# A two-layer hybrid DeltaNet / S5 / MLA / MoE block on one core: a timeline simulation as the list scheduler's machine, and another merge order for the first mixer

## The chip, the cores and the metric

The kernel runs on one NeuronCore of a Trainium2 chip. The metric is the device time of one execution in microseconds (us), as the median of several runs.

## The reference, cut to what matters

There are 256 latent tokens and 256 context tokens of width 1024, and two layers. Every sub-layer is RMS norm, a shift and scale that come from a conditioning vector through a large matrix (`ada_w`, 2 x 1024 x 6144), the work itself, and a gated residual.

```
for i in range(2):
    sh1, sc1, g1, sh2, sc2, g2 = adaln(c, ada_w[i], ada_b[i])        # and the same for c_ctx
    h_l, h_c = modulate(x, ...), modulate(ctx, ...)
    if i == 0: o_c, o_l = mixer_ab(h_c, h_l, ...)   # gated DeltaNet (4 heads, two directions) beside S5 (32 groups)
    else:      _, o_l = mixer_mla(h_c, h_l, ...)    # latent attention, 8 heads
    x = x + g1 * o_l
    x = x + g2 * grouped_moe(modulate(x, ...))      # 16 experts, top 2, f32 weights
    # in layer 0 the same two lines for ctx
return rmsnorm(x, final_norm_g)
```

The DeltaNet heads project the input to q, k, v, z, pass q, k, v through a convolution over 5 tokens, normalize k, build decay matrices for each of 4 token tiles and 2 directions, solve a triangular system in each tile, and scan over the tiles. The S5 groups are a linear recurrence over time with a gated output (`glu`).

## The kernel before, in words

**Stages.** The kernel is written in a tile framework: each statement issues one instruction on one engine, and the framework adds the semaphores and the buffer slots. In the order of the program:

1. `norm0` and the first third of layer 0's conditioning (`ada_gen(0, 0)`), then the input projection of the S5 part (`proj_u`) beside the first quarter of the S5 tables.
2. The first mixer's projections, tables, S5 recurrences and decay matrices, as five streams that are merged (below), with the last 72 loads of `ada_w` as the fifth.
3. Triangular solves and the scan (`solve`, `scan`, `dn_out`).
4. The output projection of layer 0 (`out_proj0`), its router, and its 16 experts (`experts0`, three fp32r passes on TensorE for each product).
5. The attention of layer 1 (`prep`, `keys`, `scores`, `values`), its output projection (`out_proj1`), the router, the experts (`experts1`, f32, two experts side by side), and the last norm.

**The merge.** `merge(order, *gens)` at the end of stage 1 takes one digit of `ORDER` after the other and runs the generator of that number up to its next `yield`; what is left goes round robin. The streams are:

- 0: `s5_run(0)` to `s5_run(3)` and `glu()`. `s5_run(q)` waits (by yielding) until the tables of quarter q are there, multiplies (`U`, `Eq`), scans on VectorE, multiplies again (`Fq`, `XC`, `Tq`) and transposes. `glu` makes four blocks; each of them holds a tile of the tag `sq` (L973) until its result is stored (L977).
- 1: `s5_tables(1)` to `s5_tables(3)`: factors `Fq`, `Eq`, and then `Tq`, which goes out to DRAM in 4 transfers (`kdd`, L579) and comes back in 8 (L583), all on the queue of SyncE (SP).
- 2: `gates`, `norm_k`, `decays` (8 steps, two for each token tile), `inverses`. A step of `decays` stores its matrices (`egd` on SP at L864, `dcd` and `atd` on ScalarE's queue at L865 and L867). `inverses` loads them back in 4 transfers on SP (`x<-atd`, L873), copies them (L874), and then runs a chain of 31 pairs on VectorE (L880, L882). It stores the result (`xvd`, L887 and L888).
- 3: `proj_k`, `proj_z`, `proj_q`, `proj_v`: 16 blocks of 128 channels, 24 matmuls each, with a load of weights (L608), a split into two fp32r parts (L602, L603) and, but for z, a convolution on VectorE (L742).
- 4: `loads`: 8 stores of zeros, then `ada_gen` for the other parts of the conditioning, 72 steps of one 512 KB load on SP and 2 matmuls (of f32, so 4 records in the trace).

`ORDER` has 224 digits: 50, 30, 30, 24 and 90 of the five streams.

**Behind the merge.** `fetch` loads the decay matrices (`A<-atd`, L1048, on SP), and 16 transfers bring the inverses into `DT` (L1040). Their tiles lie where tiles of the merge lay, so they wait until those are given up.

**The second output projection.** `out_proj1` multiplies in two column halves (`n` = 0, 1; 48 matmuls `ps<-ch,oT` each). Between them it calls `moe_open`, which loads `cols<-modd` (L1323, 8 KB, on ScalarE's queue; in it, each element of 4 bytes has an address of its own) and multiplies it with the router's matrix (`ps<-rw,cols`, 8 matmuls of f32, 16 records).

**What sets the order on an engine.** Each engine runs its instructions in a fixed order, and so does each DMA queue: an instruction whose semaphore has not come holds all those behind it. The framework finds this order when the program is complete. It is a list scheduler: it plays the program on a simulated machine, and whenever an engine of that machine is free it takes the instruction with the lowest number in program order among those whose inputs are ready there. So both matter, the program's order (`ORDER` for the merge) and what the simulated machine holds to be ready. The machine is by default the functional core simulator. With `schedule_with_timeline_sim=True` (L2187) it is a timeline simulation, in which every instruction is a list of events that hold engines, queues and other devices, for which instructions contend. Where the program demands an order, it says so with `issue_after`.

Of the kernel before, what the change touches and what calls it, by code (L numbers as in the profile page):

```python
# [38 lines left out]
ARB = 3  # L39
EA = 0  # L40
HG = (2, 5)
ORDER = "40124430441043014410430044034041140224222234140404134042104340241432100440412304401424034102444031420440134204140344014042231440204144304214040321444142300041204344012034140402430142440423041422241143444000003444432444444444"


def const_arrays():
# [115 lines left out]
def _build(es, tc, I, O):  # L161
# [156 lines left out]
    def merge(order, *gens):  # L318

        for c in order:  # L320
            next(gens[int(c)], None)
        rr(*gens)
# [5 lines left out]
    def seq(*gens):  # L328
        for g in gens:
            yield from g  # L330
# [632 lines left out]
    def glu():  # L963
        gluw = [load_chunk(I["glu_w"][:, n * 256:(n + 1) * 256].rearrange("(k p) n -> p k n", p=128), [128, 4, 256])
                for n in range(2)]
        glub = gp.tile([128, 4], F32, name="glub")
        nc.sync.dma_start(glub, I["glu_b"])
        V.tensor_scalar(glub, glub, 0.5, None, op0=OP.mult)
        for b in range(4):
            p = ps(1)  # L970
            for k in range(4):
                mm(p, gluw[b // 2][:, k, b % 2 * 128:b % 2 * 128 + 128], yT[:, k, :], k == 0, k == 3)
            th = d2.tile([128, 512], F32, tag="sq", bufs=2, name=nm("gth"))  # L973
            S.activation(th, p, AF.Tanh, scale=0.5, bias=glub[:, b:b + 1])
            V.tensor_scalar(th, th, 0.5, 0.5, op0=OP.mult, op1=OP.add)
            V.tensor_tensor(th, yT[:, b, :], th, op=OP.mult)
            G.dma_start(c5d[b], th)  # L977
            yield
# [13 lines left out]
    with tc.issue_after(mark.ins):  # L992
        G.memset(X, 0.0)
        rr(with_loads(proj_u()), s5_tables(0))
    yT = pj.tile([128, 4, 512], F32, tag="uy", name="yT")
    merge(ORDER,
          seq(s5_run(0), s5_run(1), s5_run(2), s5_run(3), glu()),
# [1193 lines left out]
```

## Time and profile before

| what | value |
|---|---|
| median of 3 runs | 1413.93 us (1410.01 to 2414.91) |
| the profiled execution's own time | 1414.94 us |
| its span, first to last instruction | 1412.7 us |
| mean granted TensorE clock | 0.942 of full speed |
| busy: TensorE matmul / VectorE / ScalarE / GpSimd | 1251.5 / 787.6 / 529.6 / 381.0 us |
| moved by DMA | 340.40 MB |

Times in the rows are from the start of the span. The span is one execution; 2.2 us lie around it. PE is TensorE's matmuls, PEld its weight loads, DVE VectorE, ACT ScalarE, POOL GpSimd, SP SyncE; "SPq" and "ACTq" are the instructions that start transfers on those two queues. A row of the timeline has start, length, engine, line, operation, output<-inputs and count, and in square brackets the idle time before it and what ended it.

### The profile page before, as it was taken

The numbers are of one execution on the slowest core, as the hardware profiler recorded it, in microseconds if no ns is written. First come the engines' busy times: TensorE is split into PE (matmuls) and PEld (weight loads), VectorE is DVE, ScalarE is ACT, GpSimd is POOL, SyncE is SP. The second block draws the span as 40 slices with busy tenths as digits, with TensorE's granted clock in tenths as the row PEclk, the third lists the DMA queues.
The fourth block names the chain that finished last, engine by engine and source line by source line (L and its number), as shares of the span: only waits on it lengthen the run. The fifth ranks groups of instructions, "written<-read, shape, count | busy, mean of one in ns | idle before, by whom it ended". The sixth has DMA issues, their size and how long they took to land. (4 is left out here: it accounts for less than half of the span.)

```text
span 1412.7 us, 18172 instructions
## 1 busy us (share of the span) xinstructions
PE 1251.5 (89%) x6716; PEld 847.8 (60%) x6716; DVE 787.6 (56%) x1460; ACT 529.6 (37%) x775; POOL 381.0 (27%) x266
## 2 busy tenths in 40 slices
PE   5889989899788999589999999976999669999996
PEld 1786655555327988457777777744777544444422
DVE  5776756844974465767775577775566151221112
ACT  3312634544112242167776477724365011000100
POOL 1443434320126330334443233353231020000000
PEclk9999999899798999789999999998999779999998
DMA  8713457767488345679999699753034569999980
GB/s 306 257 34 88 155 171 221 225 216 235 149 251 281 131 172 180 273 244 345 377 369 330 227 317 358 283 210 113 32 135 155 194 254 385 398 401 400 399 336 31
DMA packets 201805, 340.40 MB, mean 241 GB/s; under 512 B 31726, under 2 KB 70638, under 8 KB 201201
## 3 DMA queue, kind: packets, MB, share of 16 engines
q1 hardware_dynamic: 171952, 310.97, 62.3%
q10 hardware_dynamic: 23920, 16.95, 3.9%
q0 software_dynamic: 5840, 11.28, 2.2%
q8 instruction: 55, 0.90, 0.3%
q14 instruction: 38, 0.30, 0.1%
HBM read 320.56 MB, written 27.82 MB: 247 GB/s over the span
## 5 line engine op out<-in xcount | busy, mean ns | idle before, releaser
L206 PE MATMUL ps<-hi,sp 128*128 128x512 f32 x816 | 269.5, 404 | 6.0 <-ACT sp L1640 3.7
L1661 DVE TENSOR_TENSOR lo<-ch,hi 128x2048 fp32r<-128x2048 f32 x80 | 185.1, 2330 | 84.6 <-ACT hi L1660 79.8
L1660 ACT ACTIVATE hi<-ch 128x2048 fp32r<-128x2048 f32 x96 | 184.1, 1920 | 80.3 <-PE ps L206 52.8
L206 PEld LDWEIGHTS ps<-hi,sp 128*128 128x128 f32 x816 | 154.0, 190 | 42.7 <-ACT sp L1640 4.4
L206 PE MATMUL ps<-lo,sp 128*128 128x512 f32 x408 | 164.9, 404 | 3.2 <-DVE lo L1661 2.4
L206 PE MATMUL ps<-ch,stat 128*32 128x512 f32 x384 | 93.9, 646 | 31.7 <-DMA ch<-in_ada_w 30.6
L206 PE MATMUL ps<-ch,xT 128*64 128x512 f32 x480 | 119.7, 596 | 0.0
L1661 POOL TENSOR_TENSOR lo<-ch,hi 128x2048 fp32r<-128x2048 f32 x16 | 73.9, 4621 | 160.6 <-ACT hi L1660 160.6
L206 PEld LDWEIGHTS ps<-lo,sp 128*128 128x128 f32 x408 | 77.8, 191 | 26.9 <-DVE lo L1661 8.8
L206 PEld LDWEIGHTS ps<-ch,xT 128*64 128x64 f32 x480 | 36.1, 137 | 66.5 <-issue 65.2
L228 POOL TENSOR_TENSOR frs<-rs,sm 128x1 f32<-128x1 f32 x2 | 1.1, 560 | 259.8 <-DVE rs L227 259.8
L1867 ACT ACTIVATE aT<-ps 128x512 f32<-128x512 f32 x8 | 4.8, 597 | 149.1 <-PE ps L203 149.1
L206 PE MATMUL ps<-ch,aT 128*64 128x512 f32 x240 | 60.0, 596 | 0.7 <-ACTq L1588 0.7
L1880 DVE TENSOR_TENSOR y<-ps,bcm 128x512 f32<-128x512 f32 x16 | 11.1, 691 | 81.8 <-PE ps L206 81.8
L603 POOL TENSOR_TENSOR wl<-raw,wh 128x1024 fp32r<-128x1024 f32 x16 | 38.7, 2417 | 66.2 <-ACT wh L602 66.0
L206 PE MATMUL ps<-hH,wh 128*128 128x512 f32 x128 | 55.0, 430 | 0.0
L206 PEld LDWEIGHTS ps<-ch,stat 128*32 128x32 f32 x384 | 13.6, 112 | 67.7 <-DMA ch<-in_ada_w 35.0
L206 PE MATMUL ps<-hL,wh 128*128 128x512 f32 x128 | 53.8, 420 | 0.0
L206 PE MATMUL ps<-hH,wl 128*128 128x512 f32 x128 | 53.1, 415 | 0.0
L742 DVE SCALAR_TENSOR_TENSOR ac<-ps,convw,ac 128x510 f32<-128x510 f32 (+1 forms) x48 | 35.5, 740 | 23.7 <-ACT ac L738 23.3
L1152 POOL TENSOR_TENSOR ch<-ch,ch 128x512 fp32r<-128x512 f32 (+1 forms) x28 | 31.1, 1127 | 58.3 <-ACT ch L1151 32.3
L206 PE MATMUL ps<-y,sT 128*128 128x512 f32 x80 | 40.9, 642 | 6.4 <-DVE y L1880 2.3
(543 smaller groups left out, 2559.7 us busy)
## 6 DMA issues: line engine op xcount, KB each, us to landing
ch<-in_wg SPq DMA_DIRECT2D x63, 1024.0 KB
ch<-in_wd SPq DMA_DIRECT2D x62, 1024.0 KB
ch<-in_wu SPq DMA_DIRECT2D x61, 1024.0 KB
ch<-in_ada_w SPq DMA_DIRECT2D x88, 512.0 KB
raw<-in_w_in SPq DMA_DIRECT2D x16, 512.0 KB
bcm<-modd ACTq DMA_DIRECT2D x12, 512.0 KB
x<-in_xs SPq DMA_DIRECT2D x8, 512.0 KB
yd<-x SPq DMA_DIRECT2D x8, 512.0 KB
```

The lines of the kernel that those rows point to most:

```text
L206: return T.matmul(out, l, r, start=start, stop=stop)
L228: G.tensor_tensor(out, t, bc(neghalf, [128, n]), op=OP.pow)
L603: eng.tensor_tensor(wl, w, wh.bitcast(F32), op=OP.subtract)
L742: V.scalar_tensor_tensor(ac[:, :, lo:hi], pv[:, :, lo + o:hi + o], convw[:, blk, j:j + 1], ac[:, :, lo:hi], op0=OP.mult, op1=OP.add)
L1152: eng.tensor_tensor(lo, src, hi.bitcast(F32), op=OP.subtract)
L1660: last_split[:] = (S.activation(hi, w, AF.Copy), eng.tensor_tensor(lo, w, hi.bitcast(F32), op=OP.subtract))
L1661: eng.tensor_tensor(lo, w, hi.bitcast(F32), op=OP.subtract))
L1867: S.activation(j.aT.rearrange("p k n -> p (k n)"), p, AF.Copy)
L1880: V.tensor_tensor(j.y[:, nh], p, g2[:, nh * 512:(nh + 1) * 512], op=OP.mult)
```

## The change

`TileContext` gets `schedule_with_timeline_sim=True`, and `ORDER` becomes another string with the same count of each digit. No instruction is added or removed, and no size changes.

```diff
-ORDER = "40124430441043014410430044034041140224222234140404134042104342240341432100440412304401424034102444031420440134204140344014042231440204144304214040321444142300041204344012034140402430142440423041422241143444000003444432444444444"
+ORDER = "34412403430144440044040300242210424344412243010024424111140334104140214400004414102414344410200402240124334343003344404201040010120044140302144444443240404244431011020444414342402413424412004334321404444044442023224044444404144"
...
-    with tile.TileContext(nc) as tc:
+    with tile.TileContext(nc, schedule_with_timeline_sim=True) as tc:
```

## Rows read from the trace of the kernel before

**Rows 1.** The page: the span, TensorE's busy time, and its clock in 40 slices.

```profile
span 1412.7 us, 18172 instructions
...
PE 1251.5 (89%) x6716; PEld 847.8 (60%) x6716; DVE 787.6 (56%) x1460; ACT 529.6 (37%) x775; POOL 381.0 (27%) x266
...
PEclk9999999899798999789999999998999779999998
```

**Rows 2.** Busy time by stretch, one line for each (stretch, its length, then as named).

```profile
core 0: us, PE busy (x) PEld busy (x) DVE busy (x) ACT busy (x) POOL busy (x), PEclk, DMA share, GB/s
58.00:428.00 370.00, 327.00 (x2125) 214.40 (x2124) 250.68 (x506) 130.02 (x227) 120.20 (x92) 0.93 0.59 181
...
365.00:410.00 45.00, 31.42 (x153) 11.81 (x154) 43.16 (x73) 4.63 (x12) 8.71 (x4) 0.81 0.55 180
...
600.00:935.00 335.00, 321.13 (x1446) 248.73 (x1445) 228.89 (x157) 235.06 (x196) 128.86 (x49) 0.98 0.86 306
935.00:1104.00 169.00, 152.48 (x680) 110.96 (x679) 101.19 (x254) 70.53 (x171) 51.37 (x46) 0.94 0.38 138
...
1160.00:1395.00 235.00, 230.16 (x1075) 92.08 (x1074) 43.26 (x81) 19.79 (x32) 0.00 (x0) 1.00 0.92 349
```

**Rows 3.** TensorE's timeline in the merged stretch: some matmuls that came after a wait.

```profile
76.64 1.11 PE L203 MATMUL ps<-cm,w 128*128 128x128 f32 x4 [4.72 <-DVE w L550]
...
191.02 1.09 PE L203 MATMUL ps<-cm,kn 128*128 128x128 f32 x4 [5.43 <-DVE kn L764]
...
272.77 2.04 PE L206 MATMUL ps<-kT 128*128 128x128 f32 x8 [5.03 <-DVE x L855]
...
381.48 1.92 PE L206 MATMUL ps<-ch,stat 128*32 128x512 f32 x4 [3.12 <-DMA ch<-in_ada_w]
...
397.05 1.05 PE L206 MATMUL ps<-ch,stat 128*32 128x512 f32 x4 [1.24 <-DMA ch<-in_ada_w]
```

**Rows 4.** Timelines of SyncE's queue, VectorE and TensorE at the end of the merge.

```profile
338.57 6.68 SPq L199 DMA_DIRECT2D ch<-in_ada_w  x2
345.35 4.21 SPq L873 DMA_DIRECT2D x<-atd  x4
349.66 2.01 SPq L579 DMA_DIRECT2D kdd<-kc  x4
351.77 1.70 SPq L199 DMA_DIRECT2D ch<-in_ada_w  x2
359.52 3.64 SPq L583 DMA_DIRECT2D Tq<-kdd  x8
...
362.80 0.68 DVE L874 COPY x<-x 64x1024 f32<-64x1024 f32 x1
...
408.98 1.05 DVE L886 COPY x<-x 128x1024 f32<-128x1024 f32 x1
...
414.43 4.56 PE L206 MATMUL ps<-yT,ch 128*128 128x512 f32 x10
...
426.59 0.69 DVE L976 TENSOR_TENSOR gth<-yT,gth 128x512 f32<-128x512 f32 x1
...
427.44 0.38 SPq L1048 DMA_DIRECT2D A<-atd  x1
...
430.41 2.04 PE L206 MATMUL ps<-DT,A 128*128 128x128 f32 x8 [4.93 <-DMA A<-atd]
```

**Rows 5.** Timelines of TensorE and ScalarE's queue in the second output projection; one stretch.

```profile
1095.71 8.71 PE L206 MATMUL ps<-ch,oT 128*128 128x512 f32 x36
...
1098.48 0.45 ACTq L1323 DMA_DIRECT2D cols<-modd  x1
...
1117.88 3.57 PE L206 MATMUL ps<-rw,cols 128*128 128x16 f32 x16 [13.46 <-DMA cols<-modd]
1121.29 7.45 PE L206 MATMUL ps<-ch,oT 128*128 128x512 f32 x24
...
1120.00:1130.00 10.00, 10.00 (x41) 8.21 (x41) 1.96 (x4) 0.59 (x1) 0.00 (x0) 0.76 0.00 0
```

More of the change, by code (lines that the diff above doesn't have):

```diff
@@ L41 @@
 HG = (2, 5)
-ORDER = "40124430441043014410430044034041140224222234140404134042104340241432100440412304401424034102444031420440134204140344014042231440204144304214040321444142300041204344012034140402430142440423041422241143444000003444432444444444"
+ORDER = "34412403430144440044040300242210424344412243010024424111140334104140214400004414102414344410200402240124334343003344404201040010120044140302144444443240404244431011020444414342402413424412004334321404044442023224044444404144"
 def const_arrays():
```

## Prediction

> **What bounds the kernel now.** I read the page first. TensorE's matmuls fill 1251.5 of 1412.7 us [rows 1], so 161.2 us of the span are without one, and the change, which takes no instruction away, can only win from those and from stretches at the lower clock. Then I cut the span into stages [rows 2]. In the merged stretch (58 to 428 us) matmuls fill 327.0 of 370.0 us: 43 us are open. In layer 0's experts it is 321.1 of 335, in the attention 152.5 of 169, so 14 and 17 us are open there. In layer 1's experts 230.2 of 235 us are filled, beside a DMA share of 0.92: that stage ends with its weights, and order gains there only if the loads start sooner. So a new order has some 80 us to work with, in many small holes. Next I looked for what ends the holes. In the first part of the merge TensorE waits for VectorE in front of a few matmuls, 4.72, 5.43 and 5.03 us long [rows 3]: the instruction at the head of the queue was not ready, and others behind it were of other streams. In the last part the reason is another: from 365 to 410 us VectorE is busy for 43.2 of 45 us and TensorE for 31.4 [rows 2], at a mean granted clock of 0.81. The chain of inverses runs there, from its first copy at 362.8 to its last at 409 us [rows 4], and TensorE has little left to do beside it but conditioning loads, for which it waits (3.12 and 1.24 us [rows 3]). Last, the longest single hole after the first load: 13.46 us in the second output projection [rows 5].
>
> **The change, part by part.** The sum is made against the profiled execution, 1414.9 us, which lies 1.0 us above the median.
>
> *The second output projection.* `cols<-modd` is issued at 1098.5 us and TensorE, done with the first column half at 1104.4, sits at the 16 records of `ps<-rw,cols` until 1117.9 [rows 5]. Behind them in its queue stand the 48 matmuls of the second half, which need nothing of `cols`; 24 of them then take 7.45 us, so all 48 take some 15 us and could fill the hole. While it lasts, the slots of the output weights stay taken: from 1120 to 1130 us the DMA share is 0.00 [rows 5], and the next experts' weights, which end the kernel, come that much later. `rw,cols` stands first by its program number, so the simulated machine must have held `cols` to be there. A machine in which the 8 KB transfer contends with the megabytes in front of it would see it later and send the second half ahead. The ends are 0 (the order stays) and -15 (the hole, and the 1.6 us by which those 24 matmuls ran over the pace of the 36 before them: 24 x (7.45/24 - 8.71/36)). I take -10, nearer to the row, since the whole wait lies on the path.
>
> By the Trainium skill (DMA: Bandwidth & Descriptors, Rules for kernel authors) a transfer whose last dimension isn't contiguous becomes one descriptor per element. The 19.4 us of this 8 KB load agree with that as well as with contention. If so, a timeline that prices it by its bytes still holds it to be early, this term is 0 and the sum would be 1412, which lies in the third rival's chance.
>
> *The stalls in the merge.* Three of them add up to 15.2 us [rows 3]. Another order loses these and makes others. The ends are -15 (none comes back) and +15 (as many come on top); a machine with better times should leave fewer, so I take -5.
>
> *The end of the merge.* Here I walked both strings through the generators and listed what stands in front of each step in program order. The last step of `decays`, on which the inverses depend, is digit 144 of the old string and 155 of the new (from 0). In front of it stand the same 14 of 16 projection blocks, the same three S5 quarters, and 46 conditioning steps before against 50 now. Then `inverses` issues its loads: before with 4 more conditioning steps and two table steps in between, now with 3, a projection block, two table steps, and the step of the third tables that puts 4 `kdd` stores and 8 `Tq` loads on SP's queue. A conditioning step is 1.05 us of TensorE [rows 3]; a block is 24 matmuls at about 0.24 us, the pace of the 36 [rows 5], so 5.8 us. So the decays end 4 steps, about 4 us, later by TensorE's work, and the loads of the inverses another 5 us (a block in place of one conditioning step) if the queues keep program order. Everything after that is a chain (loads, 46 us of VectorE, `xvd`, `DT`), and less of TensorE's work is left to cover it: two blocks went with it before, one does now. The ends are 0 (the chain starts when the decays end, and they end no later) and +16 (those 9 us, and 7 of idle time at the lower clock). I take +7. That last part also holds `glu`: the solver's first load waited for its last block (426.6, then `A<-atd` at 427.4 [rows 4]); in the new string all four blocks stand behind the inverses where two did before, but nothing else then stands in their way, so I cost it at nothing and keep it for the rival below.
>
> *Everything else* (solves, experts, attention): the same program numbers on another machine. The open time is 14 and 17 us in the two longest stages [rows 2]; most of it is at their ends, where no other work is ready. The ends are -15 (half of it) and +20 (a weight load that comes late once or twice; a conditioning load that was late cost 3.12 us and left the next matmuls at 1.92 instead of 1.05 us, the lower of the clock's two levels, 1.2 instead of 2.4 GHz [rows 3]). I take -5.
>
> Together -10 - 5 + 7 - 5 = -13, and 1414.9 - 13 = 1402 us.
>
> **The rivals.** *Slower: the inverses' loads fall in behind `Tq` on SP.* That queue is in order. Before, `x<-atd` went out at 345.4 and the `kdd`/`Tq` transfers after it; these held the queue from 349.7 to 363.2 us, as `Tq` had to wait for `kdd` to land [rows 4]. In the new program order they stand ahead of `x<-atd`. If the scheduler keeps that, the chain starts 13.5 us later on top of the 4 us of the decays, and behind `x<-atd` the later conditioning and `glu_w` loads wait too, which leaves TensorE idle at 1.2 GHz and brings the four `glu` blocks, all behind the chain, to the end: two more of 8 records at 0.456 us, 7.3 us in all [rows 4]. 13.5 + 4 + 7.3 = 24.8, with nothing gained elsewhere and about 3 us of clock, gives 1443. It decides when the chain starts more than about 17 us later in its stage than before. For it speaks the order of the strings; against it that the scheduler takes what is ready, and that `x<-atd` needs only `atd`.
>
> The Trainium skill (DMA: Bandwidth & Descriptors, Anatomy of one DMA) says that a wait for a semaphore happens on the sequencer that issues, before dispatch, so a waiting transfer holds the queue. The trace agrees: two issues filled 6.68 us, where one alone takes 0.38 [rows 4]. By this rule alone the sum above would be 13.5 us higher, about 1415.
>
> *Faster: the holes go.* If the simulated times are near the real ones, the hole in the output projection goes whole (-15), the three stalls and most of their like go (-15), the other stages give 10, and the tail gains as much as the later start costs. That is -40, 1375; with some new stalls 1380. The 43 open us in the merge and the 0.81 clock speak for it; against it speaks that most of the rest (routers, first load, last norm) is dependent work.
>
> *It hardly does what it says.* Outside the merge the order may come out nearly as before, `cols` included, as most instructions are ready in their program order. Then only the new string acts: -5 + 7, 1417.
>
> **How the numbers follow.** The forecast, 1402, gets 0.36; the case that little changes, 1417, 0.18; the faster one 0.27; the slower one 0.19. A measurement of this kernel can tell about 2%, 28 us, from no change: below 1386 is faster, above 1442 slower. So faster has 0.27, same 0.54, slower 0.19. The forecast's own range is 1386 to 1422. To hold 8 in 10 I take in most of the faster case, down to 1370, and much of the slower, up to 1440: all ends at once would be 1370 and 1466, but they are of four separate terms.
>
> **What would show it.** Right: `rw,cols` after at least some of the second half's matmuls, and the hole in front of it below 5 us; layer 1's experts starting some 10 us earlier against the end of the attention; in the merge the first copy of the inverses some 4 to 10 us later, with the solver's first matmul near 435 us. Wrong: the hole still at 13 us; `x<-atd` behind `Tq` and the solver after 445 us; or a new wait of TensorE for a weight chunk in the experts of layer 0, which would make that stage longer than its 335 us. I would be most wrong if the other machine moved loads on SP's queue past each other in the experts, which no row of before can show.

## The result, and where the time went

The changed kernel takes 1393.9 us (median of 4 runs, 1392.8 to 1394.3), where the kernel before took 1411.4 us in the runs beside it (median of three; a fourth, at 2414.9 us, is left out and nothing on record explains it): a ratio of 0.987, 95% interval 0.985 to 0.989. By 2% that is no change; it is still some 1.3% faster, and the interval excludes 1. The forecast of 1402 us is 8 us above it, and the time lies inside the range. The reasons, though, were wrong in both directions, and the rest of this text is about that.

The page of the kernel after, for [rows 1]: matmuls are busy for 23.5 us less, though none was removed, and the span is 20.2 us shorter.

```profile
span 1392.5 us, 18176 instructions
...
PE 1228.0 (88%) x6716; PEld 842.5 (61%) x6716; DVE 780.7 (56%) x1460; ACT 515.7 (37%) x764; POOL 382.9 (28%) x266
...
PEclk9899999999789998799999999987999869999999
```

Stretches of the kernel after, cut at its own stages, for [rows 2] (columns as there). The merge has 321.5 us of matmuls in 339 us now; the experts of layer 0 still have their 323.5, but take 350 us for them where it was 335.

```profile
53.00:392.00 339.00, 321.52 (x2174) 215.09 (x2174) 251.83 (x525) 119.47 (x223) 122.46 (x95) 0.96 0.66 204
...
582.00:932.00 350.00, 323.54 (x1420) 253.37 (x1420) 224.93 (x150) 231.22 (x193) 127.49 (x48) 0.98 0.82 289
932.00:1093.00 161.00, 145.58 (x659) 106.65 (x660) 97.02 (x251) 70.76 (x171) 45.63 (x44) 0.94 0.35 124
1147.00:1380.00 233.00, 230.75 (x1089) 95.43 (x1088) 45.31 (x84) 19.79 (x32) 0.00 (x0) 1.00 0.93 352
```

To see where 20 us came from I took the same marks from the timelines of every kernel of this study: the first projection matmul (`ps<-wh,hH`), the solver's first matmul (`ps<-DT,A`), the first router product (`ps<-rt,onesB`), the first and last matmul of layer 0's experts (`ps<-hi,sp`), the first and last of the second output projection (`ps<-ch,oT`), and those of layer 1's experts (`ps<-ch,xT`, `ps<-ch,aT`). Lengths between them, us, each from one profiled execution (executions of one kernel spread by 1.6 to 20 us here, so a difference of a few us in one row may be chance):

| stage | before | after | difference |
|---|---|---|---|
| start to first projection (preamble) | 44.9 | 53.4 | +8.5 |
| to the solver's first matmul (merge) | 385.5 | 345.3 | -40.2 |
| to the router (solves, first output projection) | 159.7 | 155.1 | -4.6 |
| to the experts' first matmul | 17.8 | 28.0 | +10.2 |
| layer 0's experts | 333.4 | 349.9 | +16.5 |
| to the second output projection (attention) | 147.8 | 146.1 | -1.7 |
| second output projection | 48.0 | 43.7 | -4.3 |
| to layer 1's experts | 23.6 | 26.0 | +2.4 |
| layer 1's experts | 239.1 | 231.8 | -7.3 |

So the merge gave 40 us, of which the preamble and the experts of layer 0 took 35 back. The merge first. What TensorE waits for between 60 and 300 us, one line for each cause (total, times, longest), first in the kernel before:

```profile
PE ps L203 <- DVE w L550: 5.9, 3, 4.7
PE ps L203 <- DVE kn L764: 5.4, 1, 5.4
PE ps L206 <- DVE x L855: 5.0, 1, 5.0
PE ps L206 <- DVE XC L935: 1.9, 1, 1.9
```

The same view of the kernel after:

```profile
PE ps L206 <- DMA ch<-in_ada_w: 2.9, 4, 1.6
PE ps L206 <- DVE x L855: 1.3, 1, 1.3
```

The three long stalls of [rows 3] are gone and hardly any took their place. From 60 to 310 us TensorE is busy for 244.3 of 250 us, where it was 229.6. The end of the merge, for [rows 4], from the timelines of SyncE's queue, VectorE and TensorE:

```profile
306.91 1.39 SPq L873 DMA_DIRECT2D x<-atd  x2
309.90 1.29 SPq L873 DMA_DIRECT2D x<-atd  x2
...
323.82 3.62 SPq L583 DMA_DIRECT2D Tq<-kdd  x8
...
318.47 0.67 DVE L874 COPY x<-x 64x1024 f32<-64x1024 f32 x1
379.48 1.05 DVE L886 COPY x<-x 128x1024 f32<-128x1024 f32 x1
390.62 0.69 DVE L976 TENSOR_TENSOR gth<-yT,gth 128x512 f32<-128x512 f32 x1
...
371.73 15.98 PE L206 MATMUL ps<-yT,ch 128*128 128x512 f32 x32
...
398.68 3.71 PE L206 MATMUL ps<-DT,A 128*128 128x128 f32 x14 [10.08 <-DMA dec<-dcd]
```

The inverses' loads go out ahead of `Tq` on SP. Their first copy is 44 us earlier than in [rows 4], their chain takes 62 us instead of 47 (VectorE still has scans to do beside it), and the last gate product, which gives up the space for `A`, comes at 391 instead of 427 us. The hole of [rows 5] shrank and did not go:

```profile
1088.81 9.89 PE L206 MATMUL ps<-ch,oT 128*128 128x512 f32 x41
...
1108.55 3.56 PE L206 MATMUL ps<-rw,cols 128*128 128x16 f32 x16 [7.62 <-DMA cols<-modd]
```

With those 41, 72 of the 96 matmuls stand ahead of `rw,cols` now, where there were 48. `cols` still takes 17.1 us to land (issued at 1091.4).

### The profile page after: what moved, and what is told of

Same layout as the page of the kernel before. It is cut to its first block, busy times and chain, and to the rows that moved or that the text cites. A ratio compares the mean times of both kernels' runs of the same rounds, so it can differ in the third digit from the quotient of the medians.

```text
span 1392.5 us, 18176 instructions
## 1 busy us (share of the span) xinstructions
PE 1228.0 (88%) x6716; PEld 842.5 (61%) x6716; DVE 780.7 (56%) x1460; ACT 515.7 (37%) x764; POOL 382.9 (28%) x266
## 5 line engine op out<-in xcount | busy, mean ns | idle before, releaser
L206 PEld LDWEIGHTS ps<-hi,sp 128*128 128x128 f32 x816 | 154.9, 192 | 62.7 <-ACT hi L1660 17.1
L206 PE MATMUL ps<-ch,xT 128*64 128x512 f32 x480 | 116.5, 595 | 0.0
L206 PE MATMUL ps<-ch,stat 128*32 128x512 f32 x384 | 90.7, 685 | 26.8 <-DVE stat L236 14.2
L1641 DVE TENSOR_TENSOR sp<-ps,sp 128x512 fp32r<-128x512 f32 x51 | 33.8, 687 | 43.8 <-ACT sp L1640 43.7
L206 PE MATMUL ps<-hH,wh 128*128 128x512 f32 x128 | 52.2, 408 | 0.6 <-DVE gab L682 0.6
L206 PE MATMUL ps<-hL,wh 128*128 128x512 f32 x128 | 50.9, 397 | 0.0
L1732 POOL DMA_INDIRECT yd<-y,rt x16 | 36.0, 2248 | 47.8 <-ACT y L1730 40.1
L280 ACT ACTIVATE junk<-x 128x1024 bf16<-128x1024 f32 x16 | 16.8, 1053 | 85.4 <-DVE x L1225 38.9
```

Of the source, the lines that this page charges most:

```text
L206: return T.matmul(out, l, r, start=start, stop=stop)
L280: S.activation(junk, src, AF.Square, accum_out=out)
L1641: V.tensor_tensor(lw, pv, h.bitcast(F32), op=OP.subtract)
L1732: G.indirect_dma_start(out=yd, in_=j.y, in_offset=None, bounds_check=1023, oob_is_err=False, out_offset=bass.IndirectOffsetOnAxis(ap=m.row ...
```

## The experiments

**Which of the two edits?** Theories before the runs: the string carries the merge's gain (A), the scheduler carries it (B), or only both together gain (C). Against the kernel after, the first run takes back the string, the second the scheduler.

```diff
-ORDER = "3441240343..."
+ORDER = "4012443044..."
```

```diff
-    with tile.TileContext(nc, schedule_with_timeline_sim=True) as tc:
+    with tile.TileContext(nc) as tc:
```

> The scheduler by the timeline simulation, with the merge order string of before. Theory A (the new string carries the merge's gain, the scheduler only moves the rest): the solver's first matmul stands near 430 to 440, the losses seen after the change stay (first projection matmul some 8 us later than before, the first layer's experts some 26 us longer than before), and the time is 1425 to 1445 us. Theory B (the scheduler carries the gain, whichever string it gets): solver's first matmul near 400, time 1390 to 1400 us. Theory C (only both together gain, each drawn for the other): as A for this kernel, 1425 us or more, but then the string alone does not gain either.

> The new merge order string, with the scheduler as before. Theory A: the solver's first matmul comes 30 us or more earlier than the 430 of before, the preamble and the experts are as before, and the time is 1375 to 1385 us, faster than with both. Theory B: the string is worth nothing alone, 1405 to 1420 us. Theory C: the string was drawn for the other scheduler and loses under this one, 1415 to 1440 us.

The scheduler alone gave 1408.3 us, ratio 0.996 (0.994 to 0.999); the string alone 1413.8 us, 1.002 (0.999 to 1.004). None of the theories had both. Lengths of the stages:

| | before | string alone | scheduler alone | both |
|---|---|---|---|---|
| preamble | 44.9 | 42.6 | 53.3 | 53.4 |
| merge | 385.5 | 387.6 | 360.7 | 345.3 |
| of it, first projection to the last matmul `ps<-cm,gg` of `decays` | 282.1 | 266.5 | 250.8 | 241.3 |
| of it, from there to the solver | 103.4 | 121.1 | 109.9 | 104.1 |
| router to experts' first matmul | 17.8 | 18.1 | 28.2 | 28.0 |
| layer 0's experts | 333.4 | 333.2 | 348.6 | 349.9 |
| second output projection | 48.0 | 47.9 | 43.2 | 43.7 |
| layer 1's experts | 239.1 | 239.1 | 231.8 | 231.8 |

Outside the merge everything, gains and losses, is the scheduler's. In the merge it gives 25 us by itself. The string gives nothing under the old scheduler and another 15 under the new one. The two added rows say where: with both edits the whole gain lies ahead of the last step of `decays`, and the rest takes as long as before. With the string alone `decays` end 15.6 us sooner after the first projection, and the rest takes 17.7 longer.

**The start of layer 0's experts.** After the change GpSimd splits an up weight (4.55 us) ahead of the gathers of the first tokens, which before went first. Timelines of GpSimd and TensorE in the kernel after:

```profile
565.79 4.55 POOL L1661 TENSOR_TENSOR lo<-ch,hi 128x2048 fp32r<-128x2048 f32 x1 [12.06 <-PE ps L206]
570.52 2.94 POOL L1627 DMA_INDIRECT xe<-h2d,rt  x1 [0.18 <-issue]
...
579.87 1.94 PE L203 MATMUL ps<-cm,xe 128*128 128x128 f32 x8 [11.07 <-DMA xe<-h2d,rt]
```

The gather's indices were ready at 563.4 us, but the split stands in front of it and itself waits until 565.8. The experiment holds the splits of the first unit's weights, this one among them, behind the second gather:

```diff
-                    half(unit(0), name, hh, first if (name, hh) == ("wg", 0) else None)
+                    with tc.issue_after(gathers[1].ins):
+                        half(unit(0), name, hh, first if (name, hh) == ("wg", 0) else None)
```

> After, with GpSimd's split of the first up weights held behind the second gather of tokens. If that split ahead of the gathers makes the hole at the start of the first layer's experts (11 us of TensorE behind the gathered tokens), the hole falls to 4 to 6 us and the time is 1386 to 1389 us. If the gathers wait for the routing anyway, 1393 to 1395 us.

1382.2 us, ratio to before 0.980 (0.975 to 0.984), a larger gain than expected. The stage is 17.6 us long, as before the change, and the wait on the tokens is gone; the rest of the kernel kept its lengths but for the attention (143.1 instead of 146.1 us, not explained). Counted from the router's first product, the first gather starts 6.8 us sooner. The same timelines:

```profile
562.80 1.10 POOL L1627 DMA_INDIRECT xe<-h2d,rt  x1 [9.98 <-DVE rt L1525]
...
566.53 4.57 POOL L1661 TENSOR_TENSOR lo<-ch,hi 128x2048 fp32r<-128x2048 f32 x1
...
567.80 0.66 PE L203 MATMUL ps<-cm,xe 128*128 128x128 f32 x4
```

**The body of layer 0's experts.** In each unit ScalarE rounds six weight chunks (`hi`, 96 in 16 units) and splits the turned activations and tokens (`sp`). Before, the activations' split stood ahead of the last rounding; after, behind it and behind the next unit's Silu. The page's groups for `ps<-hi,sp` (busy, mean, idle before and its cause), kernel after:

```profile
L206 PE MATMUL ps<-hi,sp 128*128 128x512 f32 x816 | 270.2, 406 | 20.5 <-ACT hi L1660 14.0
```

One unit of it on ScalarE and TensorE:

```profile
643.04 1.91 ACT L1660 ACTIVATE hi<-ch 128x2048 fp32r<-128x2048 f32 x1 [0.88 <-PE ps L206]
644.86 0.58 ACT L1713 ACTIVATE act<-ps 128x512 f32<-128x512 f32 x1
645.34 1.08 ACT L1640 ACTIVATE sp<-ps 128x512 fp32r<-128x512 f32 x2
...
645.01 0.50 PE L206 MATMUL ps<-hi,sp 128*128 128x512 f32 x1 [1.13 <-ACT hi L1660]
645.98 0.50 PE L206 MATMUL ps<-hi,sp 128*128 128x512 f32 x1 [0.47 <-ACT sp L1640]
```

```diff
-                    half(nxt, "wu", 0)
+                    with tc.issue_after(last_sp["a"].ins):
+                        half(nxt, "wu", 0)
...
-                    gated(j)
+                    with tc.issue_after(last_sp["x"].ins):
+                        gated(j)
```

> After, with one order laid down in the first layer's experts: on ScalarE the split of a unit's turned activations goes ahead of the rounding of the next unit's first half of the up weights, and the next unit's Silu behind its turned tokens, as it was before the change. If that place on ScalarE is what lengthens the body of these experts (waits of 1.1 and 0.5 us of TensorE at each of 14 units), the stage is 12 to 18 us shorter and the time 1376 to 1382 us. If the waits come from something else (the turned tokens' transposes that now stand ahead on TensorE), they stay with another releaser: 1390 to 1395 us.

1375.8 us, 0.974 (0.969 to 0.979): the stage takes 328.3 us, less than the 333.4 of before and a little less than expected. The merge came out 5 us longer in this execution (1379.7 us, the longest of the four), though no line of it was touched. TensorE's instructions in it come in the same order as after, so that is a difference between executions and not a new order. The group and the unit with this order:

```profile
L206 PE MATMUL ps<-hi,sp 128*128 128x512 f32 x816 | 264.7, 402 | 5.5 <-ACT sp L1640 4.8
...
644.18 0.60 ACT L1640 ACTIVATE sp<-ps 128x512 fp32r<-128x512 f32 x1 [1.31 <-PE ps L203]
644.67 1.91 ACT L1660 ACTIVATE hi<-ch 128x2048 fp32r<-128x2048 f32 x1
```

So both losses in these experts are places in one engine's fixed order. At one, the gather is 6.8 us later, 4.55 of them for the split itself. At the other, TensorE waits 20.4 us in all in the kernel after (12 times for `hi`, 13 times for `sp`). In front of `ps<-hi,sp` 15.0 us of idle time went, and the stage's matmuls are busy for some 5 us less (323.5 and 318.7 us), which together is most of the 21.6 us by which the stage fell. The edit sets two orders at once; what each is worth was not taken apart.

**The preamble: a miss.** After the change ScalarE issues five parameter loads ahead of the Silu of the conditioning vector instead of three (it starts at 13.74 instead of 9.07 us), VectorE does S5 parameters ahead of the conditioning's sum, and all scalings of `x` stand ahead of the first rounding into `hH`. TensorE's timeline in the kernel after:

```profile
47.11 0.66 PE L203 MATMUL ps<-cm,adaev 128*128 128x128 f32 x4 [3.77 <-DVE adaev L262]
53.36 0.60 PE L206 MATMUL ps<-wh,hH 128*128 128x256 f32 x1 [5.59 <-ACT hH L658]
```

The experiment puts the loads and the norm's squares behind the Silu and staggers the scalings.

```diff
+    with tc.issue_after(silu.ins):
+        nc.scalar.dma_start(convw.rearrange("p a b -> p (a b)"), I["conv_w"])
...
-        rr(norm0(), ada_gen(0, 0))
+        with tc.issue_after(silu.ins):
+            rr(norm0(), ada_gen(0, 0))
```

> After, with three orders of before laid down in the preamble: on ScalarE the parameter loads (convolution, S5) and the norm's squares behind the Silu of the conditioning vector, and the scaling of each projection chunk two chunks behind the rounding. If these orders made the preamble 8.5 us longer, the first projection matmul moves from 53.4 to 45 to 48 us and the time is 1386 to 1390 us. If the merge hides a late start (its streams then wait for something else), the first matmul moves and the time stays at 1392 to 1395 us. If the preamble is bound by the conditioning weights alone, nothing moves.

1405.8 us, 0.996 (0.994 to 0.999), 12 us worse than the kernel after. The first projection moved the wrong way, to 56.1 us: with all loads ahead of the squares, TensorE waits for the normed input. And the merge behind it came out at 357.6 us, 12 longer, with another order of its instructions on TensorE. The wait for the normed input:

```profile
25.31 1.97 PE L203 MATMUL ps<-cm,x 128*128 128x128 f32 x8 [9.24 <-ACT x L635]
```

What each of the three places costs stays open, as my order was no better than the scheduler's.

**The tail of the merge: a misread wait.** In the run of the scheduler alone the third tanh of the GLU came 8 us after the GLU's matmuls, and the trace put its wait down to `DT<-xvd`, whose loads stood before it on ScalarE's queue. ScalarE and its queue in that run:

```profile
395.58 7.79 ACTq L1040 DMA_DIRECT2D DT<-xvd  x4
403.50 0.69 ACT L974 ACTIVATE gth<-ps,glub 128x512 f32<-128x512 f32 x1 [15.02 <-DMA DT<-xvd]
```

Two kernels hold those loads behind the last tanh, with the old and with the new string.

```diff
+                with tc.issue_after(tanh[0].ins):
                     (nc.scalar if j else nc.sync).dma_start(
                         DT[s_, j, 4 * d:4 * d + 4]...
```

> Machine alone (old string, scheduler by the timeline simulation), with the loads of DT from xvd held behind the last tanh of the GLU. In the run of the machine alone ScalarE held four of these loads for 7.8 us in front of the third tanh, and the last gate product came at 407.8 us though the GLU's matmuls ended at 395. Theory T (most of what the new string gains over the old one under this scheduler is this one place): the solver's first load of A moves from 409 to 397 to 400 us, and the time is 1396 to 1400 us. Theory S (the string's gain lies in the streams before the GLU): the load moves by 3 us at most, 1404 to 1409 us.

> After, with the same hold of the loads of DT. There the loads stand between the tanhs and cost some 3 us (last GLU matmul at 386.9, last gate product at 390.6 us). Theory T: solver's first load 2 to 4 us earlier, 1389 to 1392 us. If DT then comes too late for the solver's first matmul, 1394 to 1398 us.

1408.0 us, 0.998 (0.996 to 1.001), and 1395.9 us, 0.988 (0.983 to 0.993): within 2 us of the same kernels without the hold. In the first, with the loads out of the way, the tanh waited all the same, and its releaser now reads:

```profile
400.05 0.69 ACT L976 ACTIVATE gth<-ps,glub 128x512 f32<-128x512 f32 x1 [12.41 <-DMA c5d<-gth]
```

It waits for a buffer: `gth` has two, and the third tanh needs the first block stored (`c5d`, 256 KB, issued at 392.4 from GpSimd's queue; the longest of the four such stores took 7.6 us to land, which would be 400.0). Theory T fell: the solver's first load of `A` moved by 3 us, to 406.0, and the time not at all, where the string is worth 15 us of the merge.

**Is the new string better, or fitted?** The two digits of every pair are exchanged, so that no step stands more than one place from where it stood.

```diff
-ORDER = "34412403430144440044..."
+ORDER = "43144230341044440044..."
```

> After, with the two digits of each pair of the new string exchanged, so that every step stands at most one place from where it stood. Theory F (the new string's gain over the old one under this scheduler is a fit to this very order): most of the 16.5 us goes, solver's first load at 400 to 410 us, 1400 to 1410 us. Theory C (the gain is in the coarse order of the streams): 392 to 397 us, 1392 to 1399 us.

1409.9 us, 0.999 (0.995 to 1.002): theory F, though the solver's first load, at 416.8 us, came later than it said. The merge is 367.1 us, longer than with the old string. TensorE is still busy for 242.8 of the 250 us from 60 to 310, but with other work: the last matmul of `decays` comes at 316.4 instead of 294.6 us, behind 14 projection blocks and 49 conditioning steps instead of 13 and 46. The inverses' first copy follows at 336.0 instead of 318.5 us and the last ends at 404.2 instead of 380.5; from `decays` to the solver it is 103.8 us, as after. So the scheduler removes the waits on VectorE with each of the three strings (between 60 and 300 us TensorE waits for VectorE 18.2 us before, and under the new scheduler 1.8, 1.9 and 2.8 us with the old, the new and the exchanged string). What the new string adds is an earlier end of `decays`, and this one shift of a place loses it; other shifts were not tried.

**Why does the string alone give nothing?** Under the old scheduler the new string does move the inverses' first copy forward by 14.6 us (348.2). But their chain then takes 61 us where it took 47, so its result goes out (`xvd`) at 407.8 us, where it was 409.0. And the GLU's weights wait for ring slots that conditioning loads hold, so the last gate product ends at 426.9 us, nearly as before. One kernel moves the last 19 conditioning steps of the string behind the GLU, ten of them from before the last S5 product, and adds five steps of stream 0; a second does the same under the new scheduler, with both orders in the experts.

```diff
-ORDER = "...44442023224044444404144"
+ORDER = "...0020232200000001" + "4" * 19
```

> String alone (scheduler of before), with ten of the conditioning steps moved from before the last S5 product to behind the GLU. Theory G (with the string alone the merge ends where it did because the GLU's weights wait for ring slots behind conditioning loads): the GLU's first matmul comes 8 to 14 us earlier than 409.7, the last gate product at 413 to 418 instead of 426.9 us, and the time is 1400 to 1408 us, unless the loads of DT now stand behind those conditioning loads on SyncE. Theory W (the work of the streams is conserved, whatever stands last): the last gate product moves by 4 us at most, 1410 to 1418 us.

> The two experts' orders together with the string of the late conditioning steps, under the new scheduler. If the GLU's weights, waiting for ring slots behind conditioning loads, end the merge (18 us between the last S5 product and the first GLU matmul after the change), the GLU starts some 8 us earlier, the solver some 5 us (the inverses end at 380), and the time is 1356 to 1362 us. If the late steps only move into the solves, it is that of the two experts' orders alone, 1362 to 1370 us; if the new string's order was a fit, 1375 us or more.

1418.1 us, 1.004 (1.001 to 1.007), and 1382.7 us, 0.978 (0.974 to 0.982), the second 14 us more than the two experts' orders without the late steps (1368.9, below). Theory G was right on the GLU and, by the exception that it names, not on the time. SyncE's queue and TensorE with the old scheduler:

```profile
387.61 2.67 SPq L199 DMA_DIRECT2D ch<-in_glu_w  x2
...
408.88 0.99 SPq L1040 DMA_DIRECT2D DT<-xvd  x2
409.95 15.04 SPq L199 DMA_DIRECT2D ch<-in_ada_w  x7
425.05 4.55 SPq L1040 DMA_DIRECT2D DT<-xvd  x6
429.71 0.42 SPq L1048 DMA_DIRECT2D A<-atd  x1
...
432.90 2.04 PE L206 MATMUL ps<-DT,A 128*128 128x128 f32 x8 [1.66 <-DMA dec<-dcd]
```

The GLU's first matmul is 13.8 us earlier (395.9) and the last gate product 12 us (414.6), but the inverses still end at 407 us, and then the moved loads hold SP's queue for 15 us in front of six of `DT`'s loads. In the other kernel `A` is loaded at 378.8 us, 14 earlier than after, and `DT` comes last again. SP's queue, ScalarE with its queue, and TensorE:

```profile
385.66 0.32 SPq L888 DMA_DIRECT2D xvd<-x  x1
...
394.47 4.68 SPq L1056 DMA_DIRECT2D Kn<-knd  x4
404.59 7.63 SPq L1040 DMA_DIRECT2D DT<-xvd  x8
...
394.27 1.09 ACT L1082 ACTIVATE qk<-ps 128x512 f32<-128x512 f32 x2 [20.88 <-DMA dec<-dcd]
401.93 10.71 ACTq L1040 DMA_DIRECT2D DT<-xvd  x8
...
412.25 2.04 PE L206 MATMUL ps<-DT,A 128*128 128x128 f32 x8 [21.17 <-DMA DT<-xvd]
```

`DT`'s loads go out 16 us after `xvd`, where after the change it was 1.7 us. That is not only a place on SP's queue: on ScalarE's, nothing stands in front of them after 395.4 us. From 380 to 402 us the DMA engines are busy throughout (share 1.02), with `A`, `dec`, `qe`, `w_out` and conditioning loads that went ahead; a late landing of `xvd` among those is the nearest reading, which no run isolates. The solver needs both, the space that the GLU gives up and the inverses in `DT`. In these two kernels, the one was moved ahead and the other ended the merge.

**Versions that beat both kernels.** First all four orders together (gathers, activations, preamble, tail), then, as the preamble's was the one that failed, the two in the experts alone.

> After, with the four orders together (gathers first, turned activations first, preamble, tail). If the places are on one path, one behind the other, the gains add: 1393.9 - 11.7 - 18.0 - 5 - 3 = 1356, so 1353 to 1362 us. If layer 1's experts, bound by their weight loads, give part of it back: 1365 to 1375 us.

> After, with the two orders in the first layer's experts alone (gathers first, turned activations first). If the loss of the merge in the run with all four orders came from the preamble's order, the merge is as after (solver's first load of A at 392 to 397 us) and the experts are as in that run (some 350 us from routing to the last expert matmul), so 1393.9 - 11.7 - 18.0 = 1364, 1362 to 1370 us. If the two experts' orders disturb the merge too, 1375 us or more.

All four: 1384.4 us, 0.980 (0.976 to 0.984), the forecast of 1356 missed by the preamble (56.3 us) and the merge (358.5). The two in the experts: 1368.9 us, 0.968 (0.964 to 0.973), 25 us under the kernel after and the fastest here; the merge stays at 343.9 us, and layer 0's experts take 17.9 + 334.2 us. That is at the upper end of what was expected: the two gains do not quite add up (25 us, where they were 11.7 and 18.0 singly), as the body takes 5.9 us more than with its order alone, for a reason not looked into.

## Why the prediction came out right, and why it should not have

*The second output projection, forecast -10, measured -4.3.* The mechanism held: another simulated machine sent matmuls of the second half ahead of `rw,cols`. I took most of the hole; 24 matmuls stayed behind it, and 7.6 of its 13.5 us remain, so over half of the gain that I read from [rows 5] was not there. Nor did the whole wait lie on the path: the next stage took 2.4 us longer, and layer 1's experts started 1.8 us sooner against the end of the attention, where I had named some 10. By the Trainium skill (DMA: Bandwidth & Descriptors, Rules for kernel authors) this load becomes one descriptor per element. A timeline that priced it by its bytes would have left this term at 0. The trace lies between: the order moved, but not far enough to cover a load that took 17.1 us. No run here tells one descriptor per element from contention.

*The stalls, forecast -5, measured about -15.* TensorE's open time from 60 to 310 us fell from 20.4 to 5.7 us; the three stalls of [rows 3] went nearly whole, which was the end that I had given to the faster rival. With the scheduler alone 15.4 us stay open, 10.0 of them behind conditioning loads; with the exchanged string it is 7.2.

*The end of the merge, forecast +7, measured some -25* (the merge's 40.2 less the 15 above). This is the step that failed worst. I took the order of the strings for TensorE's: 46 conditioning steps and 14 projection blocks ahead of the last step of `decays` with the old string, 50 and 14 with the new one, so `decays` 4 us later. By the trace TensorE ran 46 and 14 ahead of it before, but 44 and 13 with the string alone and 46 and 13 with both edits. The stretches from the first projection matmul to the last one of `decays`, for these three kernels (columns as in [rows 2]):

```profile
44.90:327.00 282.10, 260.75 (x1729) 188.62 (x1730) 187.32 (x381) 113.27 (x202) 106.81 (x81) 0.94 0.54 171
...
42.60:309.00 266.40, 244.26 (x1697) 180.38 (x1698) 189.03 (x377) 105.14 (x194) 104.39 (x81) 0.95 0.53 171
...
53.40:294.60 241.20, 237.65 (x1705) 174.87 (x1706) 174.59 (x369) 98.57 (x185) 104.50 (x80) 0.98 0.60 191
```

With the string alone the stretch is some 16 us shorter, though as much of it is open (22.1 and 21.4 us) and TensorE waits for VectorE nearly as long as before (17.3 and 18.2 us from 60 to 300 us). So what moved `decays` there was not the waits of [rows 3]. With both edits it is some 41 us shorter, and 3.6 us of it are open. The chain behind it, which I had charged with another 5 us and idle time, takes as long as before (104.1 and 103.4 us). So all that the merge won lies ahead of `decays`, and my split into stalls and end is not one that the trace knows. How much of it is less work ahead, how much fewer waits and how much the clock (0.94, 0.95 and 0.98 of full speed in these stretches), no run takes apart. "A block in place of one conditioning step" counts what stands ahead in the program, while the schedulers had sent other work ahead.

*Everything else, forecast -5, measured +24* (the other rows of the first table). I had put the ends at -15 and +20 and thought of weight loads that come late. My sign of being wrong, layer 0's experts longer than 335 us, came true, but not through a load: the two places there are ScalarE's and GpSimd's orders in front of a TensorE whose next instruction waits for them. I had read the 14 open us of that stage [rows 2] as what another order could win, and had no term for what it could lose: a stage that is 96% full can mostly lose.

*The sum.* The merge was mis-sized by 42 us in one direction and the rest by about 35 in the other (5.7 in the projection, 29 elsewhere), so that -13 came near -20.6 is luck. Of the marks that I had named, `rw,cols` behind part of the second half came true, and `x<-atd` did not fall in behind `Tq`; the first copy 4 to 10 us later, the solver near 435 us, a hole below 5 us and layer 1's experts 10 us sooner did not come. The slower rival's mechanism, loads behind others that wait on SP, did not act in the change itself. It did in the first of the two kernels with late loads, at 15 us. What the Trainium skill says there (DMA: Bandwidth & Descriptors, Anatomy of one DMA: the wait is on the sequencer that issues) agrees with that row, seven loads that filled 15.04 us of SP's queue.

*What stays open.* Why the preamble is 8.5 us longer is known only from the order of its instructions, as the one experiment on it failed. Why the timeline simulation orders the merge better and these experts worse was not tried; that its durations are nearer to the chip's in one place and not in the other is only an argument. So is how much another drawing of the string would give. Why layer 1's experts take 7.3 us less under the new scheduler, in every kernel, was not looked into.

## What to carry to other kernels

A scheduler is judged by stage, not by the total: a change that moves the end by 20 us had moved stages by -40 and +35, and the 25 us of the losing stage came back with two ordering constraints read from the trace. Look for a ready TensorE behind one engine's fixed order (a long split ahead of a gather, a rounding ahead of what the next matmul needs), and state that order. A merge order that gains can be fitted to its surroundings: here the exchange of neighbours cost 22 us of the merge and an edit ahead of it 12, while the edits behind it left TensorE's order in it as it was. So after an edit look at that stage again. And where a buffer, a queue and a chain end at one point, as here, moving one ahead may buy nothing until the next is moved as well.

## What the runs showed of the hardware that I had not expected

A named releaser is only the last event: the third tanh read as 15 us behind `DT<-xvd`, and with those loads gone it read as 12.4 us behind a 256 KB store, 3.5 us sooner. Starts of loads from ScalarE's queue had no fixed distance: in the preamble of the kernel after, starts of ScalarE's loads from L384 to L411 lie 1.4 to 2.3 us apart, in the kernel before those from L409 to L415 0.4 to 0.5 us. SyncE's queue issued weight loads beside both, so what makes the difference is open.
